# One scores run and one values run a head pair, shorter roots, a different first feed

## The chip, the cores and the metric

The kernel runs on one core of a Trainium2 chip. The metric is the device time of one execution in microseconds; the time before is the median of three runs. Engines are named TensorE (PE, with its weight loads as PEld), VectorE (DVE), ScalarE (ACT), GpSimd (POOL) and SyncE (SP); SP, ACT and POOL also issue DMA transfers on queues of their own.

## The reference

One encoder layer over 512 positions of 2048 channels, float32 throughout:

```python
xn = rms_norm(x, attn_norm_g)
u_val, u_gate, q, k, v = split(xn @ w_in)         # 1024 columns each
y_conv = silu(layer_norm(depthwise_conv(u_val * sigmoid(u_gate), width=31)))
y_na = neighborhood_attention(q, k, v, rpb)       # 16 heads of 64, 8 x 64 grid, window 8 x 16
x = x + concat(rms_norm(y_conv), rms_norm(y_na)) @ w_out
xn = rms_norm(x, ffn_norm_g)
gate, val = split(depthwise_conv(xn @ w_up, width=3))   # 5632 columns each
x = x + (silu(gate) * val) @ w_down
return rms_norm(x, final_norm_g)
```

The grid has 8 rows and the window is 8 rows high, so every position sees all rows; in the columns it sees 16.

## The kernel before

Activations lie with channels on the 128 partitions and the 512 positions along the free axis. A float32 product is made of three products in the reduced format fp32r: `weights high x data high`, `weights high x data low`, `weights low x data high`. ScalarE makes the high part (`whi`, L126, a rounding copy) and VectorE the low part (`wlo`, L127, a subtraction) of each weight unit of 128x1024. A unit of eight 128x128 blocks is so used in 24 products of 512 columns (`group`, L146 to L154).

Opening. `split_x` (L263) loads one of 16 row blocks of x (transposed, 128x512, 2 KB a row) and splits it; `piece` (L272) loads small pieces of the first two weight columns, gate column 0 and value column 0; `first_glu` (L354) multiplies them block by block, 96 products. Squares of x for the first norm are summed on ScalarE (L309).

First stage. The string `ORDER` (L59) puts eight convolution pairs (`a`) and eight head pairs (`q`) in a row. `project` (L334) makes one column block of `w_in` out of two units; after each unit `tick` (L158) advances one generator of small steps (`steps`, `asteps`), whose instructions may be issued only behind that unit's last product. In the convolution branch `gated` (L367) multiplies by the first norm's root `rstd` and runs 31 steps of the width-31 convolution on VectorE (`y`, L380 and L384).

Attention. `attend` (L450) is such a generator for a head pair. The 64 columns are cut in four blocks of 16; each has a key window of 32 columns by 8 rows, 256 keys. `scores(b0)` multiplies queries and keys for two blocks and both heads in full float32 (L470, four products, eight passes), adds the bias table (L478), takes the maximum (L480), exponentials on ScalarE (L483), reciprocal (L484) and the normalising copy (L486). `turn()` transposes a batch (L498, eight transposes, `trp`) and ScalarE evicts it (L503). `values(b0)` multiplies with the values (L512, `vt`, eight products, sixteen passes). In time the yields give: values' transposes (`trv`, L458); scores of blocks 0 and 1; one unit with nothing; scores of blocks 2 and 3 and the first turn; values 0 and 1; second turn; values 2 and 3. A scores tile takes the two PSUM banks of tag `sc`, transposes those of tag `tr`.

Norms. `root_steps` (L232) makes a reciprocal square root: Sqrt on ScalarE, then reciprocal and one Newton step on VectorE; the 512 values are put on the diagonal of `dg` and spread to all partitions by one float32 product with `ones` (L248). It is used five times: first norm, layer norm, the two group norms, second norm.

Later stages. `out_half` multiplies with `w_out`, `up` (L706) with `w_up` and `product2` (L837) with `w_down`, the last two with seven instead of eight block products (Strassen's scheme, `TURN`, `TURN2`). `operand` (L783) prepares an operand of the closing products out of the hidden blocks; `again` (L809), called behind the products of the last hidden block, loads hidden blocks back and makes the first two operands early. `again` is called with `at`, the place in `TURN`.

End. `ready` (L893) adds the last product and the residual and sums squares, `write` (L905) makes the root out of the four partial sums (reduce, Sqrt, two scalings, reciprocal, Newton step), scales and stores.

Which instruction stands where on an engine is decided at build time by a scheduler with priorities (`shifted`) and issue conditions; `pin` keeps the written order.

Of the kernel before, what the change touches and what calls it, by code (L numbers as in the profile page):

```python
# [16 lines left out]
P = 128  # L17
D = 2048
S = 512
# [53 lines left out]
@with_exitstack  # L73
def layer(ctx: ExitStack, tc: tile.TileContext, xT, xn, w_in, w_out, w_up, w_down, par, tab, g3, out):
    nc = tc.nc
# [31 lines left out]
    ones = consts.tile([P, P], F32, name="ones")  # L107
    nc.vector.memset(ones, 1.0)
# [3 lines left out]
    for _ in range(WARM):  # L112
        nc.tensor.matmul(ps[:, :P], ones, ones, start=True, stop=True)
    eps = consts.tile([P, 1], F32, name="eps")
    nc.vector.memset(eps, EPS)
    ident = consts.tile([P, P], F32, name="ident")
# [115 lines left out]
    def root_steps(sums, n, name):  # L232

        v, r, y = (sm.tile([P, S // P], F32, tag="rs" + c, name="rs" + c) for c in "vry")
        nc.vector.tensor_scalar(v, sums, 1.0 / n, EPS, op0=ALU.mult, op1=ALU.add)
# [12 lines left out]
        nc.tensor.matmul(ps, ones, dg, start=True, stop=True)  # L248
        res = t2(name)
        nc.scalar.activation(res, ps, AF.Copy)  # L250
        return res
# [10 lines left out]
    pin = tc.keep_in_program_order  # L262
    def split_x(k):  # L263
        x1.append(t2("x"))
        i = pin(nc.sync.dma_start(x1[k], xT[k]))
        h, l = t2("xh", F32R), t2("xl", F32R)
        pin(nc.scalar.activation(h, x1[k], AF.Copy, scale=g1[:, k:k + 1]))
        pin(nc.vector.scalar_tensor_tensor(l, x1[k], g1[:, k:k + 1], h.bitcast(F32), op0=ALU.mult, op1=ALU.subtract))
        xs.append((h, l))
        return i  # L270

    def piece(n, k0, k1):  # L272
        m = (k1 - k0) * P
        raw, hi, lo = t2("we")[:, :m], t2("weh", F32R)[:, :m], t2("wel", F32R)[:, :m]
        pin(nc.sync.dma_start(raw, w_in[n, :, k0 * P:k1 * P]))
        pin(nc.scalar.activation(hi, raw, AF.Copy))
        pin(nc.vector.tensor_sub(lo, raw, hi.bitcast(F32)))
        return [(hi, lo, k - k0) for k in range(k0, k1)]

    early = [[] for _ in range(4)]  # L280
    for ks, ws in (((0,), (0, 2)), ((1,), (2, 4)), ((2, 3), (4, 8)), (range(4, 8), ())):
        for k in ks:
            split_x(k)
        for j, n in enumerate((NC_, 0)):
            if ws:
                early[j] += piece(n, *ws)
    for j, n in enumerate((NC_, 0)):
        raw, i = raw_unit(w_in[n, :, U * P:2 * U * P], U * P)
        pin(i)
        w = parts(raw, U * P)  # L290
        pin(w[2])
        pin(w[3])
        early[2 + j] = [w[:2] + (k,) for k in range(U)]
    for k in range(U, KD):
        split_x(k)
    squares = sm.tile([P, S // P, 2], F32, tag="ss", name="ss")
# [13 lines left out]
    last = pin(nc.sync.dma_start(prm, par))  # L310
    for i in range(len(early)):
        plan.append(lambda i=i: early[i])
    a_, q_ = iter(range(NC_)), iter(range(NP_))
# [40 lines left out]
    def first_glu():  # L354
        two = [psa.tile([P, S], F32, tag="tr", name="pj", bufs=2) for _ in range(2)]
        for u in range(KD // U):
            ws = weights(), weights()
            for k in range(U):
                kk = u * U + k
                for ps, w in zip(two, ws):  # L360
                    hi, lo, at = w[k]
                    m = mm3(ps, (hi, lo), at, xs[kk][0], xs[kk][1], kk == 0, kk == KD - 1)
            for _ in range(2):
                tick(m)
        late.append(lambda: gated(0, *two))
# [84 lines left out]
    def attend(p, q, k, v):  # L450
# [13 lines left out]

        def scores(b0):
            both = psa.tile([P, 2, 2, 2 * P], F32, tag="sc", name="sc")
            for i in range(2):
                b = b0 + i
                for j, hp in enumerate(hps):
                    m = nc.tensor.matmul(both[:, j, i, :], q[hp, b * P:(b + 1) * P], grid(k, KC0[b], KW)[hp],  # L470
                                         start=True, stop=True)
                    if i or j:
                        pin(m)
            two = tabs.pop(0)
            for j in range(2):
                tb = two[:, j]
                s = t2("s").rearrange("p (i k) -> p i k", i=2)
                nc.vector.scalar_tensor_tensor(s, both[:, j], DH ** -0.5, tb, op0=ALU.mult, op1=ALU.add)  # L478
# [5 lines left out]
                nc.vector.reciprocal(su, su)  # L484
                for i in range(2):
                    nc.scalar.activation(s[:, i], s[:, i], AF.Copy, scale=su[:, i:i + 1])  # L486
                soft.append(s)

        pts = []

        def turn():
            pts.clear()
            for j in range(2):
                s = soft.pop(0)
                ps = psa.tile([P, 4, P], F32, tag="tr", name="trp", bufs=2)
                for i in range(2):
                    for ch in range(2):
                        m = nc.tensor.transpose(ps[:, 2 * i + ch, :], s[:, i, ch * P:(ch + 1) * P], ident)  # L498
                        if i or j or ch:
                            pin(m)  # L500
# [4 lines left out]

        def values(b0):
            for i in range(2):
                b = b0 + i
                for ch in range(2):
                    for j in (1, 0):  # L510
                        hp = hps[j]
                        m = nc.tensor.matmul(grid(po, b * BLK, BLK)[hp], vt[b // 2][:, 2 * (b % 2) + ch, hp],  # L512
                                             pts[j][:, 2 * i + ch, :], start=(ch == 0), stop=(ch == 1))
                        if (i, ch, j) != (0, 0, 1):
                            pin(m)
# [22 lines left out]
        yield  # L538
        values(2)
        ao = t2("ao")  # L540
# [22 lines left out]
    for d in range(KD):  # L563
        xk = t2("x2")
        nc.sync.dma_start(xk, xT[d])
        x2.append(xk)
# [326 lines left out]
    def ready(x, ps, th, dh, only=range(2 * Q), fused=()):  # L893

        for i in only:
            t, d = divmod(i, Q)
            d += Q * dh
            add(x[i], x[i], ps[i])
            q = t2("sq")
            nc.scalar.activation(q, x[i], AF.Square, accum_out=sq[th][:, t, d:d + 1])  # L900
            if i not in fused:
                nc.vector.tensor_mul(x[i], x[i], gs[d])
            yield

    def write(th, t, ys, fused=()):  # L905
        v, r, y = (sm.tile([P, 1], F32, tag="rs" + c, name="rs" + c) for c in "vry")
        nc.vector.tensor_reduce(v, sq[th][:, t], axis=AX.X, op=ALU.add)
# [49 lines left out]
    for i in product2(5, a, False):  # L957
        with shifted(-100):
            for _ in ready(e3, a, 0, 0, (i,), fused):
                pass  # L960
        if i % Q == Q - 1:
            for _ in write(0, i // Q, (e3, e0), fused):
                pass
# [62 lines left out]
```

## Time and profile before

| | us |
|---|---|
| median of 3 runs | 1992.7 |
| lowest, highest | 1992.6, 1993.33 |
| the profiled execution | 1993.17 |
| its span, first to last instruction | 1991.4 |
| TensorE busy in it | 1976.7 (99%) |
| VectorE, ScalarE, GpSimd busy | 1593.1, 1100.4, 225.4 |

A span is the time between the first and the last instruction of the profile; the device time also holds what lies around it. In a row of groups, `x` is the count, then busy time and mean duration, then the engine's idle time ahead of these instructions and what ended it. In a timeline row stand start, duration, engine, line, operation, tiles and, in brackets, the idle time before it. A chain is followed back from the last instruction.

### The profile page before, as it was taken

How to read it: one execution, taken by the hardware profiler on the slowest of the kernel's cores; microseconds unless marked ns; L12 is line 12 of the kernel's file. 1: busy time of each engine (PE TensorE's matmuls, PEld its weight loads, DVE VectorE, ACT ScalarE, POOL GpSimd, SP SyncE). 2: the span in 40 equal slices, each digit the busy share in tenths (PEclk: the TensorE clock that was granted, in tenths of full speed). 3: DMA queues.
4: the chain of work that ended last, by engine and by line, in shares of the span. 5: the costliest groups of instructions: out<-in, count | busy, mean ns of one | idle time of the engine just before them, and what ended most of it. 6: DMA issues, size and time to landing. Idle time of an engine off the chain costs nothing.

```text
span 1991.4 us, 28519 instructions
## 1 busy us (share of the span) xinstructions
PE 1976.7 (99%) x10525; PEld 1685.7 (85%) x10525; DVE 1593.1 (80%) x2296; ACT 1100.4 (55%) x1728; POOL 225.4 (11%) x310
## 2 busy tenths in 40 slices
PE   9999999999999999999999999999999999999998
PEld 7878888887788888989898898989898888888886
DVE  5995798498547888888888888888888898886764
ACT  7244423438525675666666666656666644554653
POOL 0111111110001111111111111111110400000000
PEclk9999999999999999999999999999999999999999
DMA  9676667666857889999999999999986967666563
GB/s 345 176 219 186 170 169 209 182 181 186 278 148 199 216 220 271 243 267 247 262 252 257 263 245 262 248 265 244 268 228 179 362 244 231 220 215 195 192 201 116
DMA packets 143117, 451.04 MB, mean 226 GB/s; under 512 B 15232, under 2 KB 23936, under 8 KB 141568
## 3 DMA queue, kind: packets, MB, share of 16 engines
q1 hardware_dynamic: 90608, 293.98, 43.2%
q0 software_dynamic: 42624, 148.92, 34.8%
q10 hardware_dynamic: 9744, 6.30, 1.0%
q8 instruction: 83, 1.36, 0.3%
q14 instruction: 58, 0.48, 0.1%
HBM read 430.27 MB, written 111.15 MB: 272 GB/s over the span
## 4 chain that ended last, share of the span: by engine, by line
PE 96%; DVE 2%; DMA 1%; ACT 0%; issue 0%; SPq 0%; DVEq 0%
PE pu L720 37%; PE pd L848 21%; PE pj L150 7%; PE pj L153 7%; PE pj L151 7%; PE po L150 3%; PE po L151 3%; PE po L153 3%; PE pu L143 2%; PE pu L142 2%; PE pu L139 2%; DVE y L384 1%; PE sc L470 1%; PE po L512 1%; PE trp L498 1%; DMA raw<-in_w_in 0%
## 5 line engine op out<-in xcount | busy, mean ns | idle before, releaser
L127 DVE TENSOR_TENSOR wlo<-raw,whi 128x1024 fp32r<-128x1024 f32 x572 | 694.6, 1222 | 285.2 <-ACT whi L126 221.4
L126 ACT ACTIVATE whi<-raw 128x1024 fp32r<-128x1024 f32 x572 | 600.7, 1058 | 572.7 <-PE pj L151 168.0
L720 PE MATMUL pu<-xc,whi 128*128 128x512 f32 x2112 | 505.5, 391 | 0.1
L720 PEld LDWEIGHTS pu<-xc,whi 128*128 128x128 f32 x2112 | 388.0, 188 | 75.3 <-DVE xc L603 0.3
L848 PE MATMUL pd<-whi,ho 128*128 128x512 f32 x1232 | 305.1, 389 | 1.4 <-DVE vl L733 1.4
L720 PEld LDWEIGHTS pu<-xc,wlo 128*128 128x128 f32 x2112 | 274.4, 191 | 10.3
L720 PE MATMUL pu<-xc,wlo 128*128 128x256 f32 x2112 | 282.3, 283 | 0.0
L848 PEld LDWEIGHTS pd<-whi,ho 128*128 128x128 f32 x1232 | 231.0, 188 | 50.3 <-DVE vl L733 1.8
L150 PE MATMUL pj<-xh,whi 128*128 128x512 f32 x608 | 241.4, 397 | 0.0
L151 PE MATMUL pj<-xl,whi 128*128 128x512 f32 x608 | 237.6, 391 | 0.0
L384 DVE SCALAR_TENSOR_TENSOR y<-ch,prm,y 128x510 f32<-128x510 f32 (+14 forms) x240 | 169.8, 739 | 3.1
L848 PE MATMUL pd<-wlo,ho 128*128 128x512 f32 x616 | 165.0, 389 | 0.0
L153 PE MATMUL pj<-xh,wlo 128*128 128x512 f32 x608 | 150.4, 389 | 0.8 <-DVE wlo L127 0.8
L729 ACT ACTIVATE pu<-pu 128x512 f32<-128x512 f32 x132 | 76.5, 580 | 121.4 <-PE pu L720 121.2
L150 PEld LDWEIGHTS pj<-xh,whi 128*128 128x128 f32 x608 | 114.2, 188 | 27.4 <-issue 4.9
L848 PEld LDWEIGHTS pd<-wlo,ho 128*128 128x128 f32 x616 | 115.6, 188 | 24.0
L153 PEld LDWEIGHTS pj<-xh,wlo 128*128 128x128 f32 x608 | 114.0, 188 | 24.9 <-DVE wlo L127 1.2
L151 PEld LDWEIGHTS pj<-xl,whi 128*128 128x128 f32 x608 | 114.2, 188 | 23.5 <-issue 1.1
L205 POOL DMA_DIRECT2D ws<-in_w_down x88 | 79.5, 904 | 363.8 <-DMA ws<-in_w_down 132.9
L664 POOL DMA_DIRECT2D raw<-in_w_up x88 | 78.0, 887 | 286.3 <-DVE wlo L127 114.5
L139 PE MATMUL pu<-xc,whi 128*128 128x256 f32 x352 | 99.6, 283 | 0.0
L142 PE MATMUL pu<-xc,whi 128*128 128x256 f32 x352 | 99.6, 283 | 0.0
(189 smaller groups left out, 2322.9 us busy)
## 6 DMA issues: line engine op xcount, KB each, us to landing
raw<-in_w_up SPq DMA_DIRECT2D x220, 512.0 KB, 5.5
ws<-in_w_down POOLq DMA_DIRECT2D x132, 512.0 KB, 6.3
raw<-in_w_up POOLq DMA_DIRECT2D x88, 512.0 KB, 8.6
raw<-ws SPq DMA_DIRECT2D x88, 512.0 KB, 3.5
raw<-in_w_in SPq DMA_DIRECT2D x78, 512.0 KB, 5.1
raw<-in_w_down SPq DMA_DIRECT2D x66, 512.0 KB, 3.7
ws<-ws POOLq DMA_DIRECT2D x44, 512.0 KB, 5.5
raw<-in_w_out SPq DMA_DIRECT2D x32, 512.0 KB, 5.4
```

Of the source, the lines that this page charges most:

```text
L126: i = nc.scalar.activation(hi[:, :n], raw[:, :n], AF.Copy)
L127: j = nc.vector.tensor_sub(lo[:, :n], raw[:, :n], hi[:, :n].bitcast(F32))
L139: i = nc.tensor.matmul(ps, hi[:, a], mh, start=start, stop=False, skip_group_check=more)
L142: nc.tensor.matmul(ps, hi[:, a], ml, start=False, stop=False, skip_group_check=more)
L150: nc.tensor.matmul(ps, hi, mh, start=first and k == 0, stop=False)
L151: nc.tensor.matmul(ps, hi, ml, start=False, stop=False)
L153: i = nc.tensor.matmul(ps, lo[:, wk * P:(wk + 1) * P], mh, start=False, stop=last and k == len(ws) - 1)
L205: nc.gpsimd.dma_start(wsum[c][k], w_down[k, {1: A21, 2: A11, 4: A11, 6: A12}[c]], accum_op=ALU.add, max_dma_last_dim=ROW)
L384: nc.vector.scalar_tensor_tensor(y[:, a:b], h[:, a + j - PAD:b + j - PAD], prm[:, o + j:o + j + 1], y[:, a:b], op0=ALU.mult, op1=ALU.add)
L664: nc.gpsimd.dma_start(a[c], w_up[f, q2], accum_op=ALU.add)
L720: i = nc.tensor.matmul(ps[:, :n], part[:, k * P:(k + 1) * P], comb[c][k][:, :n], start=j == 0 and not more, stop=j == 2 * U - 1, skip_grou ...
L848: m = nc.tensor.matmul(ps[i], h[:, o + t * P:o + (t + 1) * P], w[:, d], start=start and not more and kind == 0 and j == 0, stop=stop and k ...
```

## The change

- Attention: scores of all four blocks are made in one run, the second two blocks into the two banks of tag `tr`; the softmax of all four tiles follows; then a yield, the first turn (into the banks of tag `sc`), a yield, the second turn, a yield, and both value products in one run. Both bias tables are loaded together.
- `root_steps`: y = 2 r / (r r + v) in place of reciprocal and Newton step; the result is split in a high and a low part, two diagonals, and spread by two fp32r products with `ones_r`.
- Opening: x comes in pairs of row blocks (128x1024, 4 KB a row) but for the first two; the first two weight columns are interleaved in `w_0` and come in pieces of 1, 1, 2, 4, 4, 4 blocks, the first three on ScalarE's queue. `first_glu` makes all high products of a piece, then its low ones.
- `again`: a third operand of the closing products is made early, behind the product at place 3.
- End: three of four partial sums are added ahead of the last one, and the root takes the rest as a bias, in fewer steps.

```diff
     g1 = consts.tile([P, KD], F32, name="g1")
     nc.scalar.dma_start(g1, par[:, :KD])
+    cuts = (0, 1, 2, 4, 8, 12, 16)
+    first = []
+    for k0, k1 in zip(cuts[:3], cuts[1:4]):
+        first.append(t2("we")[:, :2 * (k1 - k0) * P])
+        nc.scalar.dma_start(first[-1], w_0[:, 2 * k0 * P:2 * k1 * P])
...
         nc.vector.tensor_scalar(v, sums, 1.0 / n, EPS, op0=ALU.mult, op1=ALU.add)
         nc.scalar.activation(r, v, AF.Sqrt)
-        nc.vector.reciprocal(r, r)
-        nc.vector.tensor_mul(y, v, r)
-        nc.vector.tensor_mul(y, y, r)
-        nc.vector.tensor_scalar(y, y, -0.5, 1.5, op0=ALU.mult, op1=ALU.add)
-        nc.vector.tensor_mul(y, y, r)
-
-        dg = t2("dg")
-        for i in range(S // P):
-            nc.vector.tensor_scalar(dg[:, i * P:(i + 1) * P], ident, y[:, i:i + 1], None, op0=ALU.mult)
+        nc.vector.tensor_mul(y, r, r)
+        nc.vector.tensor_add(y, y, v)
+        nc.vector.reciprocal(y, y)
+        nc.vector.scalar_tensor_tensor(y, y, 2.0, r, op0=ALU.mult, op1=ALU.mult)
+        nc.vector.tensor_copy(h, y)
+        nc.vector.tensor_sub(v, y, h.bitcast(F32))
+
+        dg = [t2("dg", F32R) for _ in range(2)]
+        for d, x in zip(dg, (h.bitcast(F32), v)):
+            for i in range(S // P):
+                nc.vector.tensor_scalar(d[:, i * P:(i + 1) * P], ident, x[:, i:i + 1], None, op0=ALU.mult)
         yield
         ps = stat()
-        nc.tensor.matmul(ps, ones, dg, start=True, stop=True)
+        for i in range(2):
+            nc.tensor.matmul(ps, ones_r, dg[i], start=i == 0, stop=i == 1)
...
+    for k in range(2):
+        x = t2("x")
+        pin(nc.sync.dma_start(x, xT[0][:, k * S:(k + 1) * S]))
+        split_x(k, x)
+        pieces.append(piece(first[k], k, k + 1))
+    for p, at in ((1, 2), (2, 3), (3, 0), (4, 4), (5, 0), (6, 5), (7, 0)):
+        x = t4([P, 2 * S], "x")
+        pin(nc.sync.dma_start(x, xT[p]))
+        for k in range(2):
+            split_x(2 * p + k, x[:, k * S:(k + 1) * S])
+        if at:
+            pieces.append(piece(first[2] if at == 2 else None, cuts[at], cuts[at + 1]))
...
+        for n, (k0, k1, hi, lo) in enumerate(pieces):
+            if n > 1:
+                weights()
+            for k in range(k0, k1):
+                for x in range(2):
+                    for i, ps in enumerate(two):
+                        o = (2 * (k - k0) + i) * P
+                        nc.tensor.matmul(ps, hi[:, o:o + P], xs[k][x], start=k == x == 0, stop=False)
+            for k in range(k0, k1):
+                for i, ps in enumerate(two):
+                    o = (2 * (k - k0) + i) * P
+                    m = nc.tensor.matmul(ps, lo[:, o:o + P], xs[k][0], start=False, stop=k == KD - 1)
+            if n > 1:
                 tick(m)
...
         table(0)
-        yield
-        scores(0)
-        yield
         table(2)
         yield
-        scores(2)
-        turn()
+        both = psa.tile([P, 2, 2, 2 * P], F32, tag="sc", name="sc")
+        both = [both[:, j] for j in range(2)]
+        more = [psa.tile([P, 2, 2 * P], F32, tag="tr", name="sc", bufs=2) for _ in range(2)]
+        scores(0, both)
+        scores(2, more, True)
+        softmax(both)
+        softmax(more)
+        yield
+        both = psa.tile([P, 2, 4, P], F32, tag="sc", name="trp")
+        turn([both[:, j] for j in range(2)])
+        yield
+        turn([psa.tile([P, 4, P], F32, tag="tr", name="trp", bufs=2) for _ in range(2)])
         yield
         values(0)
-        yield
-        turn()
-        yield
-        values(2)
+        values(2, True)
...
     def again(at, i):
-        if at == 1:
-            pre.extend(operand(TURN2[0], k) for k in order2[:KEEP // 2])
+        if at in (1, 3):
+            pre.extend(operand(TURN2[0], k) for k in order2[len(pre):KEEP // 2 + (at > 1)])
...
-        nc.vector.tensor_reduce(v, sq[th][:, t], axis=AX.X, op=ALU.add)
-        nc.scalar.activation(r, v, AF.Sqrt, scale=1.0 / D, bias=eps)
-        nc.vector.tensor_scalar(v, v, 1.0 / D, EPS, op0=ALU.mult, op1=ALU.add)
-        nc.vector.reciprocal(r, r)
-        nc.vector.scalar_tensor_tensor(y, v, r, r, op0=ALU.mult, op1=ALU.mult)
-        nc.vector.tensor_scalar(y, y, -0.5, 1.5, op0=ALU.mult, op1=ALU.add)
-        nc.vector.tensor_mul(y, y, r)
+        last = sq[th][:, t, 2 * Q - 1:]
+        nc.scalar.activation(r, last, AF.Sqrt, scale=1.0 / D, bias=most)
+        nc.vector.tensor_scalar(v, last, 1.0 / D, most, op0=ALU.mult, op1=ALU.add)
+        nc.vector.scalar_tensor_tensor(v, r, r, v, op0=ALU.mult, op1=ALU.add)
+        nc.vector.reciprocal(v, v)
+        nc.vector.tensor_scalar(y, v, r, 2.0, op0=ALU.mult, op1=ALU.mult)
```

In the program as built, TensorE has per head pair 0 to 5: `trv` x8; 24 products; scores x8; 24 products; four transposes; 4 to 6 products; four transposes; the rest of 24; eight transposes; 24 products; values x16. In pairs 6 and 7 the transposes stand in pieces of two and four.

More of the change, by code (lines that the diff above doesn't have):

```diff
@@ L287, in layer, with piece @@
[L287 to L290, printed above, removed]
+    def piece(raw, k0, k1):
+        if k1 - k0 > 2:
+            raw, i = raw_unit(w_0[:, 2 * k0 * P:2 * k1 * P], 2 * (k1 - k0) * P)
+            pin(i)
+            w = parts(raw, 2 * (k1 - k0) * P)
+        else:
+            w = t2("weh", F32R)[:, :2 * (k1 - k0) * P], t2("wel", F32R)[:, :2 * (k1 - k0) * P]
+            w += nc.scalar.activation(w[0], raw, AF.Copy), nc.vector.tensor_sub(w[1], raw, w[0].bitcast(F32))
@@ L291, in layer @@
         pin(w[2])
         pin(w[3])
[L293 to L295 removed]
+        return k0, k1, w[0], w[1]
+    pieces, early = [], []
+    for k in range(2):
[10 more added lines that the diff above has]
+            pieces.append(piece(first[2] if at == 2 else None, cuts[at], cuts[at + 1]))
@@ L310, in layer @@
     last = pin(nc.sync.dma_start(prm, par))
-    for i in range(len(early)):
-        plan.append(lambda i=i: early[i])
+    for i in range(6):
+        plan.append(lambda i=i: early[i - 4] if i > 3 else None)
     a_, q_ = iter(range(NC_)), iter(range(NP_))
@@ L463, in attend, with scores @@
         soft = []
-        def scores(b0):
-            both = psa.tile([P, 2, 2, 2 * P], F32, tag="sc", name="sc")
+        def scores(b0, both, more=False):
             for i in range(2):
@@ L489, in attend, with turn @@
         pts = []
-        def turn():
-            pts.clear()
+        def turn(two, more=False):
             for j in range(2):
-                s = soft.pop(0)
-                ps = psa.tile([P, 4, P], F32, tag="tr", name="trp", bufs=2)
+                s, ps = soft.pop(0), two[j]
                 for i in range(2):
```

77 lines of the change are left out of this document (32 added, 45 removed).

## The prediction

> **What bounds the kernel now.** I read the page first, then TensorE's waits, the chain of waits in order of time, the windows by stage, the groups by form, and last the timelines of the softmax, of the hand-over to the closing products and of the end.
>
> ```profile
> span 1991.4 us, 28519 instructions
> PE 1976.7 (99%) x10525; PEld 1685.7 (85%) x10525; DVE 1593.1 (80%) x2296; ACT 1100.4 (55%) x1728; POOL 225.4 (11%) x310
> PE 96%; DVE 2%; DMA 1%; ACT 0%; issue 0%; SPq 0%; DVEq 0%
> ```
> ```profile
> PE pj L139 <- ACT xh L267: 1.6, 2, 0.9
> PE pd L848 <- DVE vl L733: 1.4, 1, 1.4
> PE pj L153 <- DVE wlo L127: 0.8, 1, 0.8
> ```
>
> TensorE is busy for 99% of the span and makes 96% of the chain. Its waits (total, times, longest) are these three and little else. So whatever costs or saves TensorE time moves the end one for one, and work on other engines counts only where TensorE comes to wait for it. The profiled execution took 1993.17 us, 1.8 over its span and 0.5 over the median of the runs, 1992.7. I sum differences against that execution and add them to the median.
>
> **The opening.** Columns: stretch, its length, busy us of PE, PEld, DVE, ACT and POOL with instructions, granted clock, DMA share, GB/s.
>
> ```profile
> 2.00:4.00 2.00, 2.00 (x12) 2.00 (x10) 0.00 (x0) 0.73 (x3) 0.00 (x0) 1.00 0.82 239
> 4.00:12.00 8.00, 7.23 (x32) 5.22 (x32) 4.49 (x9) 4.80 (x9) 0.00 (x0) 1.00 0.90 279
> 12.00:20.00 8.00, 6.81 (x29) 5.00 (x28) 6.68 (x9) 7.06 (x10) 0.00 (x0) 1.00 1.05 403
> 5.25:30.97 25.72, 23.69 (x100) 17.71 (x98) 16.83 (x25) 20.28 (x32) 0.00 (x0) 1.00 1.01 373
> 42.00:101.00 59.00, 58.94 (x259) 48.09 (x257) 54.40 (x78) 16.20 (x17) 7.21 (x10) 1.00 0.69 190
> ```
> ```profile
> 34.76 1.81 PE pj L153 x8
> 40.20 1.81 PE pj L153 x8
> 42.01 0.86 PE st L248 x2
> 46.54 1.81 PE pj L153 x8
> ```
>
> Twenty-four products of 512 columns take 40.20 - 34.76 = 5.44 us, 0.227 each. The first gate and value pair has 96 products, 21.8 us; its first starts at 5.25 and the next pair's at 30.97, 25.72 later: 3.9 us were lost to data. The same bytes come after the change, in fewer transfers: 1.57 MB until row block 3 is complete, 2.62 MB until weights 4 to 7 are there. At the 279 GB/s of the stretch from 4 to 12 us, after 2 x 239 = 0.48 MB by 4 us, they land at about 7.9 and 11.7 us. TensorE is through blocks 0 and 1 at 5.25 + 12 x 0.227 = 8.0 and through 2 and 3 at 10.7, so it waits twice for transfer and the splits behind it, about 2.5 us together instead of 3.9: **-1.4**. At 403 GB/s from the start all 3.9 go; if the 512 KB pairs of x delay the weights behind them (0.26 MB more ahead of block 2, 0.9 us), the opening is 1 us longer. Bounds -3.7 and +1.0. ScalarE now issues three weight transfers ahead of its table load; its first split waits for g1's transfer, issued before them on the same queue, so nothing is charged.
>
> [...] The trace shows 256 KB transfers of x in both stretches, 279 and 403 GB/s, so here the size alone does not set the rate and the row stands.
>
> **Roots.** A root's broadcast is one full-precision product of two passes. It stretches the 5.44 to 46.54 - 40.20 = 6.34: 0.90. Two products in the reduced form are two ordinary ones, 0.45. Five roots: 5 x 0.45 = 2.2; **-2.0**, since some come where TensorE waits anyhow. The shorter VectorE chain before it lies beside other work.
>
> The first root also loses something. In the built program its two products do not stand together: the second comes eight projection products after the first, 8 x 0.227 = 1.8 us. The gate's multiply waits for that result, and behind it on VectorE stand all the convolution steps and the weights' low parts. VectorE is 54.40 of 59.0 us busy from there to 101 us, and the wait for wlo above (0.8 us) ends that stretch. A later start cannot be caught up: the wait grows by 1.2 to 1.8; **+1.7**.
>
> **Runs of small products.** Rows of the chain around head pair 0, then the groups (busy | mean ns).
>
> ```profile
> 119.25 1.81 PE pj L153 x8
> 121.06 1.06 PE sc L470 x8
> 125.98 1.81 PE pj L153 x8
> 131.42 1.81 PE pj L153 x8
> 138.99 1.81 PE pj L153 x8
> 145.68 1.82 PE pj L153 x8
> 152.01 1.81 PE pj L153 x8
> ...
> 490.65 1.81 PE pj L153 x8
> 498.52 1.82 PE pj L153 x8
> ```
> ```profile
> L470 PE MATMUL sc<-k,q 64*128 64x256 f32 x128 | 18.2, 402 | 0.0
> L498 PE MATMUL trp<-ident,s 128*128 128x128 f32 x128 | 17.5, 276 | 0.0
> L512 PE MATMUL po<-pt,vt 128*64 128x128 f32 x256 | 17.5, 279 | 0.0
> ```
>
> Over 5.44, a scores run costs 125.98 - 119.25 - 5.44 = 1.29, scores with transposes 2.13, a values run 1.25, transposes alone 0.89. A scores run is busy 18.2 / 16 = 1.14 us; four pairs of passes at (1.14 - 0.40) / 3 = 0.246 make 0.98, so 0.31 is the fixed price of a run. Values: 1.09 a run, eight pairs at 0.116 make 0.93, fixed 0.32. Transposes: 0.93 as well, fixed nothing. In the built program all 8 pairs have one scores run and 7 have one values run (pair 6 keeps two): 15 x 0.32 = **-4.8**, to -5.6 if a run's slow first and last product count more than I can see. Against it, the first turn does not stay whole: its two heads stand 5 or 6 products apart in pairs 0 to 5, and in pairs 6 and 7 the turns fall into pieces of two and four. That is 17 pieces more. The one turn cut in three in the trace costs 498.52 - 490.65 - 7.57 = 0.30 for two extra pieces, waits included; I take 0.05 a piece between 0 and 0.15: **+0.9**.
>
> **The wait that the change adds.** Before, a turn comes 48 products and a run after its scores; after, its first head's transposes stand 24 products behind the joint scores run, 5.44 us, and the second head's 5 products and four transposes later, 7.0 us. How long the softmax takes now (ScalarE's normalising copies, one row a head, and the start of the scores):
>
> ```profile
> 166.84 1.06 PE sc L470 x8
> 329.12 1.06 PE sc L470 x8
> ```
> ```profile
> 124.70 1.28 DVE L478 SCALAR_TENSOR_TENSOR s<-sc,tab 128x512 f32<-128x512 f32 x2
> ```
> ```profile
> 129.32 0.91 ACT L486 ACTIVATE s<-s,su 128x256 f32<-128x256 f32 x2 [1.12 <-DVE su L484]
> 131.67 0.91 ACT L486 ACTIVATE s<-s,su 128x256 f32<-128x256 f32 x2
> 171.48 0.89 ACT L486 ACTIVATE s<-s,su 128x256 f32<-128x256 f32 x2
> 173.72 0.89 ACT L486 ACTIVATE s<-s,su 128x256 f32<-128x256 f32 x2
> 335.90 0.91 ACT L486 ACTIVATE s<-s,su 128x256 f32<-128x256 f32 x2 [1.09 <-DVE su L484]
> 338.15 0.89 ACT L486 ACTIVATE s<-s,su 128x256 f32<-128x256 f32 x2
> ```
>
> From the end of the scores (122.12, 167.90, 330.18) the two heads are ready after 8.1 and 10.5 us in pair 0, 4.5 and 6.7 in pair 1, 6.6 and 8.9 in pair 3. Pairs 0 and 3 are late because convolution steps and a low part stand before the bias add on VectorE (124.70, 2.6 us after the scores); the built order keeps three convolution steps, a low part and one more step there. All this was covered by 48 products; 24 do not cover it. Two shifts about cancel: the first two tiles are complete halfway through the joint run (0.9 earlier), but four tiles share VectorE and ScalarE, and the second batch's adds and exponentials stand between the first batch's steps (about 1 later). Pair 0 then waits 8.1 - 5.4 = 2.7 and for its second head 0.8 more, with its second turn 4; pair 3 waits 1.2, 0.7 and about 0.7 in its second turn, 2.6; pairs 1, 2, 4 and 5 wait 0.5 each for the second head; pairs 6 and 7, whose turns stand in pieces, 1 each. With 4 + 2.6 + 2 + 2 and some restarts: **+10**, between 3 (pairs 0 and 3 alone, caught up in part) and 17. The second table is now loaded beside the first, one transfer earlier on SP's queue ahead of weights and one more of the nine buffers held; with a DMA share of 0.69 in the last stretch above, nothing is charged. Behind a waiting transpose stand the projection products; behind those, ScalarE's weight casts wait for buffers, so the delay is not made up later.
>
> **Hand-over and end.**
>
> ```profile
> 1565.33 1.20 PE L848 MATMUL pd<-whi,ho 128*128 128x512 f32 x4 [1.41 <-DVE vl L733]
> ...
> 1568.94 0.71 ACT L801 ACTIVATE ho<-h 128x256 fp32r<-128x256 f32 x2
> ```
> ```profile
> 1984.15 0.16 DVE L907 TENSOR_REDUCE rsv<-sq 128x1 f32<-128x4 f32 x1 [0.79 <-ACT sq L900]
> 1985.57 0.75 DVE L921 SCALAR_TENSOR_TENSOR xr<-xr,rsy,g 128x512 f32<-128x512 f32 x1
> ```
>
> A third operand made early puts 18 products instead of 12 ahead of the banks that are waited for: 6 x 0.227 = 1.4 us more cover, and the 1.41 goes. But the fourth operand is cut on ScalarE only at 1568.94, behind the last block's steps, and TensorE now asks for it 1.4 earlier: the wait moves there. **0**, between -1.4 and +0.3. At the end 1.42 us pass from the reduce to the first scaling in seven dependent steps; three go at about 0.2: **-0.6**.
>
> Sum: -1.4 - 2.0 + 1.7 - 4.8 + 0.9 + 10 + 0 - 0.6 = +3.8; I take +3.5, the runs' saving being rather above 4.8. 1992.7 + 3.5 = **1996.2 us**.
>
> **Rivals.**
> *The cover holds (faster).* If the joint run lets the adds start so early that both heads are ready within 5.4 and 7.0 us, only pairs 0 and 3 wait, 3 us instead of 10: 1989.2, and 1987 with a good opening. For it: pair 1's 4.5 and 6.7. Against: pair 0's 8.1. It decides at the copies' end 5.4 us after the scores. 0.15.
> *VectorE's backlog grows.* Each wait postpones the weights' low parts too, and pairs 6 and 7 (beside the group's norms) wait 3 instead of 1, pairs 1 to 5 over 1: 16 us of waits, 2002.2. For it: VectorE's 54.40 of 59; against: every wait also gives VectorE time. 0.12.
> *The opening gets longer.* +1.0 instead of -1.4: 1998.6. 0.10.
> *The pace drops after the long wait.* No TensorE wait in the trace passes 1.4 us and the granted clock stays 1.00 in every stretch shown; pair 0's would be about 4. If the products after it ran at half pace for as long, 4 us, 2 us are lost: 1998.2. 0.05. [...]
> *The runs are not joined*, so that nothing is gained: excluded for scores, since the built order has them as one; for the turns it is counted above.
>
> **How the numbers follow.** About 0.2%, 4 us, is what a measurement of this kernel can tell from no change: under 1988.7 is faster, over 1996.7 slower. The forecast has 0.58: with waits of 8 to 12 and the opening as it may be it lies between 1993 and 1999, 0.32 of it within and 0.26 slower. The cover's case gives 0.09 faster and 0.06 within, the backlog 0.12 slower, the longer opening 0.08 slower and 0.02 within, the pace 0.04 slower and 0.01 within. Together faster 0.09, within 0.41, slower 0.50. The range runs from the cover's case, 1989.0, to the backlog's lower part, 2000.5; the forecast's own is 1993 to 1999.
>
> **What would show it.** Right: TensorE waits for ScalarE's copies before transposes, 3 to 4 us in pair 0, in total 8 to 12; its wait for wlo near 100 us at 2 to 3; one scores run of about 2 us a pair; fp32 broadcasts gone; the wait of 1.41 gone and one like it some 8 us later; first projection pair over by 29 to 30 us. Wrong: transposes without waits (then it is faster), or a first pair that ends after 31 us.

## The result, and the profile after

| | before | after |
|---|---|---|
| median of 12 runs each, us | 1992.67 | 1997.28 |
| lowest, highest | 1992.19, 1993.33 | 1996.7, 1998.24 |
| the profiled execution | 1993.17 | 1996.94 |
| its span | 1991.4 | 1995.2 |

The ratio is 1.0023, with a 95% interval of 1.0015 to 1.0031: the changed kernel is slower by about 4.6 us. The forecast was 1996.2. The page of the changed kernel and its TensorE waits (total, times, longest):

```profile
span 1995.2 us, 28529 instructions
PE 1974.7 (99%) x10525; PEld 1690.1 (85%) x10525; DVE 1596.7 (80%) x2318; ACT 1097.7 (55%) x1726; POOL 225.4 (11%) x310
PE 88%; DVE 7%; ACT 2%; issue 1%; DMA 1%; ACTq 0%; DVEq 0%; SPq 0%
```
```profile
PE trp L509 <- ACT s L499: 2.7, 3, 1.9
PE pj L157 <- DVE wlo L131: 2.5, 1, 2.5
PE trp L509 <- ACT pt L514: 1.6, 4, 0.7
PE pj L370 <- ACT weh L285: 1.3, 2, 0.7
PE pd L863 <- DVE ho L817: 1.3, 1, 1.3
PE sc L481 <- ACT ra L258: 0.8, 1, 0.8
```

TensorE has 2.0 us less work and yet the end comes 3.8 us later. VectorE, 2% of the chain before, is 7% of it now: from 68 to 132 us the chain runs over VectorE's convolution steps. Two waits are long, for a low part of the weights (`wlo`) and for the softmax of pair 0 (`s`). Behind each something else happens, which the windows show (columns as in the prediction; the clock is the seventh value):

```profile
4.00:12.00 8.00, 6.69 (x28) 5.23 (x28) 5.09 (x9) 5.49 (x11) 0.00 (x0) 1.00 0.97 371
5.78:29.79 24.01, 22.70 (x99) 18.16 (x98) 15.96 (x22) 19.38 (x30) 0.00 (x0) 1.00 1.02 405
...
101.00:102.00 1.00, 0.18 (x1) 0.18 (x2) 1.00 (x2) 0.15 (x1) 0.00 (x0) 0.91 0.00 0
103.00:104.00 1.00, 1.00 (x4) 0.81 (x3) 1.00 (x2) 0.00 (x0) 0.00 (x0) 0.50 0.68 246
...
132.00:133.00 1.00, 0.68 (x4) 0.48 (x5) 1.00 (x4) 1.00 (x4) 0.00 (x0) 0.77 0.52 162
```

The granted clock falls to 0.50 behind both waits. By the trace's record of it the slow stretches run from 101.81 to 105.22 and from 132.53 to 135.94, 3.41 us each; the shares of 0.91 and 0.77 at their edges say the same. Pair 0 on TensorE:

```profile
120.79 1.97 PE L157 MATMUL pj<-xh,wlo 128*128 128x512 f32 x8
122.69 2.00 PE L481 MATMUL sc<-k,q 64*128 64x256 f32 x16
128.42 1.98 PE L157 MATMUL pj<-xh,wlo 128*128 128x512 f32 x8
132.32 1.09 PE L509 MATMUL trp<-ident,s 128*128 128x128 f32 x4 [1.92 <-ACT s L499]
133.63 0.63 PE L155 MATMUL pj<-xl,whi 128*128 128x512 f32 x1
134.06 0.63 PE L154 MATMUL pj<-xh,whi 128*128 128x512 f32 x1
134.91 1.05 PE L509 MATMUL trp<-ident,s 128*128 128x128 f32 x4
...
144.94 1.98 PE L157 MATMUL pj<-xh,wlo 128*128 128x512 f32 x8
146.85 1.97 PE L523 MATMUL po<-pt,vt 128*64 128x128 f32 x32
...
152.50 1.98 PE L157 MATMUL pj<-xh,wlo 128*128 128x512 f32 x8
```

One scores run of 16 passes and one values run of 32, as built. Behind the wait two products start 134.06 - 133.63 = 0.43 us apart instead of 0.227, and the four transposes at 134.91 take 1.05 us; four take 0.60 in pair 2, where the clock is 1.00.

### The profile page after: what moved, and what is told of

It is laid out like the page before. It is cut to its first block, busy times and chain, and to the rows that moved or that the text cites. A ratio compares the mean times of both kernels' runs of the same rounds, so it can differ in the third digit from the quotient of the medians.

```text
span 1995.2 us, 28529 instructions
## 1 busy us (share of the span) xinstructions
PE 1974.7 (99%) x10525; PEld 1690.1 (85%) x10525; DVE 1596.7 (80%) x2318; ACT 1097.7 (55%) x1726; POOL 225.4 (11%) x310
## 4 chain that ended last, share of the span: by engine, by line
PE 88%; DVE 7%; ACT 2%; issue 1%; DMA 1%; ACTq 0%; DVEq 0%; SPq 0%
PE pu L735 37%; PE pd L863 20%; PE pj L157 5%; PE pj L154 5%; PE pj L155 5%; DVE y L396 3%; PE po L157 3%; PE po L154 3%; PE po L155 3%; PE pu L143 2%; PE pu L147 2%; PE pu L146 2%; DVE wlo L131 1%; PE po L523 1%; PE trp L509 1%
## 5 line engine op out<-in xcount | busy, mean ns | idle before, releaser
L735 PE MATMUL pu<-xc,wlo 128*128 128x256 f32 x2112 | 282.3, 283 | 0.0
L396 DVE SCALAR_TENSOR_TENSOR y<-ch,prm,y 128x505 f32<-128x505 f32 (+14 forms) x240 | 169.8, 737 | 3.1
L143 PE MATMUL pu<-xc,whi 128*128 128x256 f32 x352 | 99.7, 283 | 0.0
L147 PE MATMUL pu<-xc,wlo 128*128 128x256 f32 x352 | 99.7, 283 | 0.0
```

The lines of the kernel that those rows point to most:

```text
L143: i = nc.tensor.matmul(ps, hi[:, a], mh, start=start, stop=False, skip_group_check=more)
L147: return nc.tensor.matmul(ps, lo[:, a], mh, start=False, stop=stop, skip_group_check=more)
L396: nc.vector.scalar_tensor_tensor(y[:, a:b], h[:, a + j - PAD:b + j - PAD], prm[:, o + j:o + j + 1], y[:, a:b], op0=ALU.mult, op1=ALU.add)
L735: i = nc.tensor.matmul(ps[:, :n], part[:, k * P:(k + 1) * P], comb[c][k][:, :n], start=j == 0 and not more, stop=j == 2 * U - 1, skip_grou ...
```

## The experiments

Each edit is made to the changed kernel unless another is named. Added lines shift the line numbers: the same transposes are L509, L513 or L530.

### The first root: is the late second product the cause?

```diff
-        rstd.append((yield from root_steps(sums, D, "rstd1")))
+        rstd.append((yield from old_root(sums, D, "rstd1")))     # root_steps of before
```

> The changed kernel with the first root alone computed in the old way (one full-precision broadcast); the four later roots keep the new way. Theory A, the forecast's step: the second of the root's two products comes late, the gate's multiply starts late, and VectorE is behind with the low part near 102 us for that reason. Then the wait for wlo there falls from 2.5 us to about 0.8, the stretch of half-speed products behind it goes too (1.5 us), the broadcast costs 0.45 more: about 2.8 us less than the changed kernel, 1994.5. Theory B: TensorE merely reaches that place earlier, by the opening's gain, while VectorE's chain cannot start earlier: the wait stays at 2 to 2.5 us, and the time at 1997 to 1998.

Measured: 1993.39 us (1.0004, interval 0.9995 to 1.0013), 3.9 less than the changed kernel. The wait for `wlo` is 0.8 us, the granted clock is 1.00 from 127 to 132 us and 0.999 in the mean (0.997 in the changed kernel), and pair 0's wait is down from 1.92 to 1.54. Theory A has the wait right; that alone does not show what delayed VectorE. So the root's two products were only moved together:

```diff
-        for d, x in zip(dg, (h.bitcast(F32), v)):
-            for i in range(S // P):
+        with shifted(-600 if name == "rstd1" else 0):
+            for d, x, i in ((d, x, i) for d, x in zip(dg, (h.bitcast(F32), v)) for i in range(S // P)):
```

> The changed kernel with the first root's eight diagonal pieces and two products given precedence, so that the second product stands three products behind the first and not eight; the order on VectorE is the same but for one low part that no longer stands among the pieces. Theory A, the forecast's step: the late second product is why VectorE is behind at 102 us. Then the gate's multiply starts about 1.1 us earlier, the wait for wlo falls from 2.5 to about 1.4 and the time to about 1995.7. Theory B: VectorE has in its queue, ahead of the second unit's multiply by its gate, one step and one low part less than with the old root, and waits there for TensorE whenever it comes early; then the earlier start is lost at 52 us, the wait for wlo stays above 2 and the time at 1997.

Measured: 1997.07 us (1.0022, 1.0013 to 1.0031), the wait for `wlo` 2.5 us as before: theory B. VectorE's timeline shows it, first of the changed kernel, then with the products close, then with the old first root, and last of the kernel before:

```profile
43.79 0.69 DVE L381 TENSOR_TENSOR gate<-pj,rstd 128x512 f32<-128x512 f32 x1 [3.07 <-ACT rstd L258]
49.50 2.28 DVE L396 SCALAR_TENSOR_TENSOR y<-ch,prm,y 128x498 f32<-128x498 f32 x3
52.23 0.69 DVE L385 TENSOR_TENSOR ch<-pj,gate 128x512 f32<-128x512 f32 x1 [0.45 <-PE pj L157]
```
```profile
42.49 0.69 DVE L381 TENSOR_TENSOR gate<-pj,rstd 128x512 f32<-128x512 f32 x1 [1.55 <-ACT rstd L258]
48.19 2.29 DVE L396 SCALAR_TENSOR_TENSOR y<-ch,prm,y 128x498 f32<-128x498 f32 x3
52.06 0.69 DVE L385 TENSOR_TENSOR ch<-pj,gate 128x512 f32<-128x512 f32 x1 [1.58 <-PE pj L157]
```
```profile
47.95 3.06 DVE L417 SCALAR_TENSOR_TENSOR y<-ch,prm,y 128x498 f32<-128x498 f32 x4
50.93 1.22 DVE L131 TENSOR_TENSOR wlo<-raw,whi 128x1024 fp32r<-128x1024 f32 x1
52.54 0.69 DVE L406 TENSOR_TENSOR ch<-pj,gate 128x512 f32<-128x512 f32 x1 [0.39 <-PE pj L157]
```
```profile
49.24 3.06 DVE L384 SCALAR_TENSOR_TENSOR y<-ch,prm,y 128x498 f32<-128x498 f32 x4
52.21 1.22 DVE L127 TENSOR_TENSOR wlo<-raw,whi 128x1024 fp32r<-128x1024 f32 x1
```

With the products close the gate's multiply starts 1.30 us earlier, but the multiply `ch` of the second unit waits for TensorE until 52.06 all the same, now 1.58 us. With the old root the built queue holds a fourth convolution step and a low part in front of that multiply, so VectorE has 3.06 + 1.22 us of work to do there, against 2.28. That is 2.00 us more work done when the multiply starts, only 0.31 later than in the changed kernel: VectorE is 1.69 us ahead there, and the wait for `wlo` is just as much shorter. The kernel before has the same order as with the old root. So it is not the late start that makes the wait longer but the order that the build gave VectorE's queue with the new root. No run changed that order alone; that it is the cause rests on this sum.

### More products between scores and turn

```diff
         softmax(more)
-        yield
+        yield; yield
```

> The changed kernel with one more group of 24 products between the joint scores run and the first turn. Theory A, the forecast's step: 24 products are too little cover and 48 are enough. Then the waits of the transposes (4.3 us together) and the half-speed products behind the longest (about 1.7) go: about 1991. Theory B: in pair 0 it is VectorE's backlog of convolution steps that holds the softmax, and its steps move back with the turn: pair 0 keeps a wait of 2 to 3 us and its half-speed stretch, the other pairs lose theirs: about 1995.

Measured: 1994.94 us (1.0013, 1.0004 to 1.0022). The time is theory B's, its cause is not. TensorE's waits, and ScalarE in pair 0:

```profile
PE trp L509 <- ACT pt L514: 3.4, 3, 2.4
PE trp L509 <- ACT s L499: 0.3, 1, 0.3
```
```profile
136.82 1.99 ACT L130 ACTIVATE whi<-raw 128x1024 fp32r<-128x1024 f32 x2
138.71 0.57 ACT L514 ACTIVATE pt<-trp 128x512 f32<-128x512 f32 x1
```

The waits for the softmax have gone from 2.7 to 0.3 us: 48 products do cover it. The 2.38 us left in pair 0 (the transposes at 139.34) are for ScalarE's eviction `pt` of the first head, which stands behind two weight casts. Both heads of the first turn now lie in one PSUM tile, and in the built program the second head's transposes carry a wait for the first head's eviction. Before, each head had a tile of its own. The second turn still has two tiles, and in pair 0 to 5 its eight transposes stand together without a wait. So this wait came with the change; the forecast had not seen it. Two tiles for the first turn were not tried, so the shared tile as its cause is argued, not shown.

### The attention of before

```diff
-    def attend(p, q, k, v):      # joint runs, as changed
+    def attend(p, q, k, v):      # the whole function of before
```

> The changed kernel with the attention schedule of before (two scores runs, two turns, two values runs a pair); opening, roots, hand-over and end stay changed. Theory A: between 108 us and 580 us the changed kernel loses about 3.1 us net (waits and slow products of some 7, runs saved 4.0). Then this takes about 1994.2. Theory B: the waits only move idle time that TensorE would have had later in any case; then this loses the runs' saving and takes 1998 to 2001.

Measured: 1992.84 us (0.9999, 0.9990 to 1.0008). Theory A has the side, not the size (1994.2): the new attention costs 1997.28 - 1992.84 = 4.4 us and not 3.1, since three of the new roots, worth 0.45 us each, lie in the same stretch and stay here. What is left of the change is no faster than the kernel before either:

```profile
98.00:102.00 4.00, 1.51 (x7) 0.94 (x6) 4.00 (x7) 0.15 (x1) 0.00 (x0) 1.00 0.32 57
102.76:106.17 3.41, 3.41 (x10) 2.66 (x9) 3.41 (x5) 0.15 (x1) 0.51 (x1) 0.50 0.86 271
```

The wait for `wlo` is 2.5 us as in the changed kernel; VectorE is busy throughout it, and a slow stretch of 3.41 us follows. Eight of the eleven times lie between 1992.71 and 1993.16 and three at 1991.16 to 1991.3: about 1.6 us, the price of one slow stretch. The mean granted clock is 0.999 in those three and 0.998 in the eight, so the three had no such stretch, as far as a mean can tell; their traces are not there.

### The order of the projections

The likeliest common cause was VectorE's backlog. One letter moves the first head pair ahead of the third gate and value pair:

```diff
-ORDER = "aaaqqaqaaaqqaqqq"
+ORDER = "aaqaqaqaaaqqaqqq"
```

> The changed kernel with one letter moved in the order of the projections: the first head pair stands ahead of the third gate and value pair. Theory A: both long waits come from VectorE's convolution steps of the third pair, queued ahead of the low parts and of the softmax. Then the wait of 2.5 us near 102 and the one of 1.9 us before pair 0's transposes fall under 1.5, their half-speed stretches (1.5 and 1.1 us) go, and the time is 1988 to 1990. Theory B, the forecast's: the first root's late second product and the 24 products of cover cause them; neither is changed here: 1995 to 1998.

Measured: 1989.62 us (0.9984, 0.9975 to 0.9992), theory A. The wait for `wlo` near 102 is gone from TensorE's list, the longest wait of pair 0 is 1.0 us and the mean granted clock 0.998 against 0.997, though the first root and the cover are as in the changed kernel:

```profile
PE trp L509 <- ACT pt L514: 2.2, 4, 1.0
PE trp L509 <- ACT s L499: 0.8, 2, 0.6
```

The same letter in the kernel before:

> The kernel before with only that letter moved. It has no half-speed stretch and waits for wlo 0.8 us near 102. Theory A: the order helps only by the waits, so it takes 0.8 to 1.1 us less: 1991.7, and the remaining 4 to 5 us of the reordered new kernel are the change's own. Theory B: the order brings something else (transfers, clock), and this comes to 1988 to 1989 too; then the change itself is worth nothing.

Measured: 1991.54 us (0.9993, 0.9984 to 1.0002), 1.2 less than before and theory A. So 1991.54 - 1989.62 = 1.9 us are the change's own, once its two long waits are gone. With the letter, the cover and the old first root:

> The changed kernel with three edits together: the first root in the old way, 24 more products between scores and first turn, and the first head pair ahead of the third gate and value pair, so that fewer convolution steps stand on VectorE before its softmax. Theory A: VectorE's backlog near 100 to 135 us is what made both long waits; no wait above 1.5 us is left, and no half-speed stretch: 1987 to 1988, faster than both kernels. Theory B: VectorE's work up to 560 us is the same and its backlog only moves into the pairs behind: waits of several us appear there, 1991 or more.

Measured: 1987.37 us (0.9973, 0.9962 to 0.9984), theory A: no wait passes 1.3 us and the mean granted clock is 0.999. Without the old first root:

> The letter moved as in the kernel with the order alone, and one more group of 24 products between scores and first turn. Theory A: the waits of pairs 1 to 5 (about 2 us) go as well, and the new first root costs no wait once VectorE is not behind: 1986.5 to 1988, at least as fast as the kernel that also had the old first root (1987.4). Theory B: the old first root was needed for that: the wait for wlo near 102 us is back and the time is about 1990.

Measured: 1987.22 us (0.9971, 0.9960 to 0.9982), theory A: the new root costs no wait where VectorE is not behind. With the letter, but the attention of before:

> The reordered new kernel with the attention schedule of before; roots, opening, hand-over and end as changed. The reordered kernel with the joint runs and the cover took 1987.2. Theory A: the joint runs save 4.0 us and the waits that are left beside them (2.6 us) take most of that back: this takes 1987.9 to 1988.6. Theory B: without waits near VectorE's backlog the joint runs keep their whole 4 us: this takes 1991.

Measured: 1988.45 us (0.9979, 0.9970 to 0.9988), theory A: the joint runs are worth 1.2 us here, not 4, since 2.5 us of waits in the attention stretch, of which the old attention has none, remain beside them, and the cut turns too. Without the added cover (1989.62) they even cost 1.2. At last the softmax with precedence, added to the kernel with the letter and the cover:

```diff
-        softmax(both)
-        softmax(more)
+        with shifted(-300):
+            softmax(both)
+            softmax(more)
```

> The reordered kernel with the cover, and the softmax's steps given precedence over others that are ready. Theory A: the waits before transposes that are left (1.8 us) come from steps ahead of the softmax on VectorE and ScalarE, and most go, the pieces of the turns in pairs 6 and 7 too: about 1986. Theory B: they come from the softmax's own chain: 1987.2 as without it.

Measured: 1986.26 us (0.9968, 0.9956 to 0.9981), the lowest of all. Theory A has the time but only part of the reason. The waits for `pt` and `s` are 1.4 and 0.3 us, against 1.5 and 0.3 without it. The starts of the same products in the two traces show where the 0.8 us are gained: all between 487 and 511 us, in pair 6. There the transposes of both turns stand in four pieces instead of six, and the values in one run of 32 passes instead of two of 16. The intervals of the two ratios overlap, but all five times (1986.01 to 1986.79) lie below the six without it (1986.84 to 1987.41).

### What makes the clock fall?

```diff
+        for k in range(5 if p == 0 else 0):
+            pin(nc.tensor.matmul(both[:, 0], xs[0][0][:, :P], xs[0][0], start=True, stop=True))
         turn([both[:, j] for j in range(2)])
```

> The changed kernel with five products of 512 columns whose result nobody reads, put ahead of pair 0's first transposes: they fill 1.1 of the 1.92 us that TensorE waits there. Theory A: the half-speed products behind that wait come from the idle time, and 0.8 us of it is too short to cause them: the wait is 0.8, the granted clock stays 1.0 there, and the kernel takes about 1.1 us less, 1996.1, although it has five products more. Theory B: the slow products come from something else at this place: the clock still falls to 0.5 there and the time is 1997 to 1998.

Measured: 1997.5 us (1.0022, 1.0013 to 1.0031). Neither theory holds as written: the time is B's. In this execution the clock stayed at 1.00, though the waits were longer:

```profile
132.17 0.83 PE L509 MATMUL trp<-ident,s 128*128 128x128 f32 x4 [2.38 <-ACT s L499]
...
135.81 0.66 PE L509 MATMUL trp<-ident,s 128*128 128x128 f32 x4 [1.65 <-ACT pt L514]
```
```profile
99.00:102.00 3.00, 0.51 (x2) 0.30 (x2) 3.00 (x5) 0.30 (x1) 0.00 (x0) 1.00 0.02 3
102.00:105.00 3.00, 3.00 (x15) 2.46 (x14) 3.00 (x4) 0.76 (x1) 0.51 (x1) 1.00 0.76 214
132.00:134.00 2.00, 1.83 (x9) 1.24 (x9) 1.96 (x5) 2.00 (x7) 0.00 (x0) 1.00 0.64 231
```

Two things follow. TensorE idles 2.49 us between 99 and 102 and the clock is 1.00 from 102 to 105, while in the changed kernel the wait of 2.49 us at the same place was followed by 0.50; so the length of this wait alone does not decide. And the first transposes start at 132.17, against 132.32 with a slow stretch ahead of them and no fillers: VectorE and ScalarE set that moment, and in the changed kernel the wait at 132 swallows what the slow stretch at 102 loses. The other executions agree: their mean granted clocks run from 0.997, which all twelve runs of the changed kernel have, to 0.999 as in the trace shown, and all eleven times lie between 1997.15 and 1997.99 in no order of the clock. To get waits of many lengths, the transposes of a turn were then held together:

```diff
-            nc.tensor.matmul(ps, hi, mh, start=first and k == 0, stop=False)
+            i = nc.tensor.matmul(ps, hi, mh, start=first and k == 0, stop=False)
+            if k == 0 and 14 < weights.at < 76:
+                pin(i)
...
+                for i in range({2: 0, 4: 1, 5: 3, 3: 0}.get(p, 0) if len(soft) == 1 else 0):
+                    nc.scalar.activation(s, s, AF.Copy)
```

> The changed kernel with the projection groups kept in program order from the 15th to the 75th, so that both heads' transposes stand together and TensorE waits for the second head; ScalarE makes one extra copy of the second head in pair 4 and three in pair 5 (the values do not change). The waits should be about 1.3, 1.8, 1.9, 1.3 and 1.8 us, and one of about 4 in pair 5. [...]

Measured: 2009.36 us in a single execution. The waits, and the clock around and behind them:

```profile
102.04 0.73 PE L159 MATMUL pj<-xh,wlo 128*128 128x512 f32 x2 [2.49 <-DVE wlo L131]
132.53 1.11 PE L513 MATMUL trp<-ident,s 128*128 128x128 f32 x4 [3.51 <-ACT s L501]
389.00 0.66 PE L513 MATMUL trp<-ident,s 128*128 128x128 f32 x4 [1.59 <-ACT pt L518]
454.34 0.66 PE L513 MATMUL trp<-ident,s 128*128 128x128 f32 x4 [3.70 <-ACT s L503]
```
```profile
102.00:105.00 3.00, 2.96 (x13) 2.47 (x14) 3.00 (x4) 1.06 (x1) 0.51 (x1) 1.00 0.60 173
131.20:134.50 3.30, 1.11 (x4) 0.60 (x4) 3.26 (x8) 2.53 (x7) 0.00 (x0) 0.50 0.90 337
134.60:137.90 3.30, 3.20 (x10) 2.72 (x11) 3.14 (x8) 3.08 (x11) 0.90 (x1) 0.50 0.24 30
386.00:390.00 4.00, 2.41 (x16) 1.88 (x15) 0.35 (x3) 4.00 (x13) 0.51 (x1) 1.00 0.70 263
455.50:458.80 3.30, 3.30 (x9) 2.51 (x9) 3.23 (x5) 2.00 (x4) 0.16 (x1) 0.50 0.77 132
```

The five waits for evictions (`pt`) make 6.8 us together, 1.8 the longest, where the five expected make 8.1; the long one came as 3.70. The clock was 0.50 from 131.2 to 137.9 us, in the last part of the wait of 3.51 and behind it, and from 455.5 to 458.8, behind the one of 3.70. It was 1.00 around the wait of 1.59 (386 to 390) and, as with the fillers, behind one of 2.49 (102 to 105). In the changed kernel waits of 2.49 and 1.92 us were followed by 0.50. So a wait of 1.92 us went with a fall in one execution and one of 2.49 with none in two others; what decides it is not shown.

## Why the prediction was right or wrong

The time and its sign came out, 1997.28 against 1996.2, and the mechanism of the largest term too, TensorE waiting for the softmax. But that term was twice too large, and that the sum is only 1.1 us off is in part luck: terms that the forecast had small or at nothing filled the gap. Of its signs the waits failed: 1.9 us in pair 0 instead of 3 to 4, and some 5 in total instead of 8 to 12. In what follows "the difference" is the start of the same product after less that before, compared at places between the terms.

**Opening**, forecast -1.4: -1.18 (first product 0.52 later, first pair 24.01 us long instead of 25.72, over at 29.79). The stretch from 4 to 12 us moved 371 GB/s instead of 279. Yet TensorE still waited 1.3 us for ScalarE's copies of the pieces, so the gain stayed near the sum's -1.4. Which change of the feed raised the rate is not shown.

**Roots**, -2.0: the difference goes from -1.18 to -1.60 up to behind the first, and by -0.45 at the second norm's, about the 0.45 forecast for each; the other three lie in the attention stretch. All broadcasts are reduced-format products now, ten of 404 ns:

```profile
L256 PE MATMUL st<-dg,ones 128*128 128x512 f32 x10 | 3.9, 404 | 0.0
```

**First root, wait for wlo**, +1.7: the wait grew from 0.8 to 2.5 us, +1.68. The size is right by luck, the step "a later start cannot be caught up" is wrong: the start was 1.3 earlier with the products close, and the wait stayed 2.5. By the sum above it is the order of VectorE's queue.

**Runs**, -4.8 and pieces, +0.9: a joint scores run costs 128.42 - 120.79 - 5.44 = 2.19 against two of 1.29, a joint values run 152.50 - 144.94 - 5.44 = 2.12 against two of 1.25. That is 0.38 saved by each, 5.7 by 15, just above the forecast's upper end. From behind the wait at 102 to the end of the attention stretch the difference grows by 3.0. Waits are 5.3 of it and slow products 1.7, so the rest is -4.0. Three roots of 0.45 are among it. What is left for the pieces is 5.7 + 1.3 - 4.0 = 3.0 taken back, not 0.9. The traces have 32 pieces against 18, 14 more (the forecast had 17), so 0.2 each and not 0.05. Pair 2, which waits for nothing, confirms it: its joint runs should save 0.77, the difference falls by 4.86 - 4.24 = 0.62, and its one cut takes the 0.15.

**Waits of the turns**, +10: the term that was mis-sized. The waits are 4.3 us, and 0.8 for pair 7's scores run. In the chain of waits the first of the two copies of pair 0's first head ends at 131.76 + 0.52, and the first transposes, which need only that one, start right behind it:

```profile
131.76 0.52 ACT s L499
```

That is 7.6 us after the scores (124.69). The second copy ends 0.4 later, at 8.0; the forecast had 8.1 for both and let the transposes wait for both. The 24 products took 5.7 us, forecast 5.4: a wait of 1.92 for 2.7. But TensorE's stream was already 1.56 late by the slow products at 102. Without them the wait is 3.5: it is 3.51 with the turns held, where no product at 102 is slow, and 2.38 behind five fillers of 0.227. So the forecast had this wait too short, not too long; a slow stretch that it did not have took the place of a part of it. Pair 0's second head, forecast at 0.8, and its second turn, at 0.5, had none, the former because TensorE's clock was 0.50 by then, up to 135.94. Pair 3 has 0.67 for 2.6: its first head and its second turn, forecast at 1.2 and 0.7, were in time. Pairs 1, 2, 4 and 5 together have 0.97 for 2.0. These waits and pair 3's are for the eviction of the first head, not for the normalising copy that the forecast named. Pairs 6 and 7 have 1.6 for 2.0, half of it that scores run.

**The pace**, a rival with 0.05: it came, twice, at waits of 1.92 and 2.49 us. The products behind lost 1.6 us at 102 (the difference goes from 0.08 to 1.64 there), which pair 0's wait took up, and in pair 0 about 1.7, half of a slow stretch. The rival asked for a wait of about 4 us and then half pace for as long; that a wait is followed by half pace of its own length was the author's assumption, which no run shows, and the trace of the kernel before has a granted clock of 1.00 from 2 to 1985 us and no wait beyond 1.4. The changed kernel showed 0.50 for 3.41 us behind each of its two longest waits; with the turns held it was 0.50 from 131.2 to 137.9 us with the wait of 3.51, and from 455.5 to 458.8 behind the one of 3.70.

**Hand-over**, 0: the 1.41 us at 1565 are gone and 1.30 come back for the fourth operand at 1576.10; the difference is 4.17 ahead of both and 4.21 behind. The wait moved as forecast. **End**, -0.6: from the last add to the first scaling 1989.19 - 1986.69 = 2.50 us, before 1985.57 - 1982.68 = 2.89, -0.39:

```profile
1576.10 1.21 PE L863 MATMUL pd<-whi,ho 128*128 128x512 f32 x4 [1.30 <-DVE ho L817]
```
```profile
1986.69 0.68 DVE L914 TENSOR_TENSOR xr<-xr,pd 128x512 f32<-128x512 f32 x1
1989.19 0.75 DVE L944 SCALAR_TENSOR_TENSOR xr<-xr,rsy,g 128x512 f32<-128x512 f32 x1
```

Sum: -1.18 - 0.42 + 1.68 + 1.56 (slow products at 102) + 2.97 (attention) - 0.45 + 0.04 - 0.4 = +3.8, as the spans say. The waits before the turns came out half as long as forecast; slow stretches and pieces filled most of what was missing. Of the rivals, the cover did not hold, the backlog did not grow and the opening got no longer; the pace was the one that came.

## What to carry to other kernels

Where one engine is near its limit ahead of a stage (VectorE 54.40 of 59 us busy before pair 0), a gain on another engine shows up as a wait there: look for what can stand elsewhere in the order before shortening the work of the engine that waits for it. One letter of the order was worth 7.7 us to the changed kernel and 1.2 to the one before. When two results share a buffer so that a run can be joined, look which reader of the first now holds up the writer of the second, and what stands ahead of that reader in its queue.

## What the hardware showed that was not expected

TensorE's granted clock fell to 0.50 for 3.41 us behind waits of 2.49 and 1.92 us in the changed kernel (from 101.81 and from 132.53 us), and behind one of about 2.5 us with the old attention (102.76 to 106.17). In the changed kernel the first cost 1.6 us on the spot, and next to nothing in the end, since TensorE would have waited for another engine just behind (pair 0's first transposes start at 132.32 with it and at 132.17 without); the second cost about 1.7. The same wait of 2.49 us was followed by a clock of 1.00 with the fillers and with the turns held; what makes the difference is not shown. A wait of 2 to 2.5 us so had a price here that changed from execution to execution, beside its own length: with the old attention, eight times lie at 1992.71 to 1993.16 us with a mean granted clock of 0.998, and three at 1991.16 to 1991.3 with 0.999.
